# Moving the first stage's low-half subtractions from GpSimd to VectorE in a one-core decoder-layer kernel

## The chip, the cores and the metric

The kernel runs on one NeuronCore of one Trainium2 chip. The metric is the device time of one execution in microseconds (us). Engines are named as in the profile: PE is TensorE (PEld its weight loads), DVE is VectorE, ACT is ScalarE, POOL is GpSimd, and SP (SPq) is SyncE, which here only issues DMAs.

## The reference

One decoder layer on 512 tokens of width 1024, all in float32:

```
mod = silu(c) @ w_ada + b_ada                      # six vectors: sh1 sc1 gt1 sh2 sc2 gt2
h   = rms_norm(x, g_norm1) * (1 + sc1) + sh1
q_lat, kv_lat, k_rope, rq, rk, rv, rg = split(h @ w_in)   # 416 latent columns, then 4 x 512
x   = x + gt1 * (concat(mla(...), retention(...)) @ w_out)
h2  = rms_norm(x, g_norm2) * (1 + sc2) + sh2
x   = x + gt2 * peer(h2, w_query, sub_keys, expert_u, expert_v)
out = rms_norm(x, g_final)
```

## The kernel before

To keep float32 accuracy on TensorE, each operand of a wide product is split into a high half in the float32r format and a low half, low = value - high. A product is then three matmuls (`mm3`, L80): high by high, high by low, low by high (L81 to L83). `split` (L73) makes both halves of a weight tile: ACT copies the high half (L76), and the engine handed to it as `lo_engine` subtracts the low half (L77). The halves sit in two rotating buffers each, `hi` and `lo`.

The change lies in the first stage, `start` (L280). It goes over the eight 128-wide slices k of the model width, and for each k does the following.

1. `h_k(k)` (L231) loads two 512 KB rows of the modulation weights (`wadaT`, L131), multiplies each with silu(c) and sums on DVE (L133), adds the bias (L237) and forms the scale (L142). PE transposes and normalises the slice of x (L241), ACT applies scale and shift (L243) and makes the high half `hh` (L244), and L245 subtracts the low half `hl`.
2. `lat_load(k // 2)` (L247), for even k, loads and splits 832 columns of the latent weights; `lat_mm` (L252) multiplies four token blocks by 416 columns.
3. `wproj_load(0, k // 4)` (L257), for k = 0 and 4, loads and splits 1024 columns of the first wide projection, and `wproj_mm` (L262) multiplies. The first projection has `ci` = 0; the seven later ones call the same function with `ci` > 0.

Low halves are divided between DVE and POOL: `hl` always on POOL; latent weights on POOL for even and on DVE for odd loads; the first projection's load 0 on POOL and load 1 on DVE. After the loop come the rotary tables (`tables`, L177, some twenty small DVE operations), the evaluation of the latents (`ev_lat`, L297, with a power on POOL at L156) and the rotation of the first projection.

The weight rows stream through three buffers named `raw`, shared by the modulation rows and the later projections. In this part SP issues DMAs in program order; a load waits in SP's queue until the buffer that it fills is released, and all later loads wait behind it. The order of instructions on the other engines is laid out ahead of time by a planner that simulates the program with its own costs for each instruction, then each engine runs its queue in that order. The stages after `start` follow an order written out by hand:

```python
ORDER = "L m0! p1 d3 p2! m1 p3 d4 p4 d2 p5 p6 r0! r1! p7 r2 r3 X0 X1! d5! m2 g! m3 w0 X3 X2 h0 w1 q0 q1! h1 q2 q3"
```

Here L is `start`, p1 to p7 are the other projections, d the other modulation vectors (eight `wadaT` rows each), m and r the attention and retention blocks, w and q the output and query projections. A dense expert stage (about 700 to 1500 us) closes the kernel.

Of the kernel before, what the change touches and what calls it, by code (L numbers as in the profile page):

```python
# [8 lines left out]
F32 = mybir.dt.float32  # L9
# [11 lines left out]
NB = 4  # L21
# [27 lines left out]
def build(ctx: ExitStack, tc: tile.TileContext, A, out):  # L49
    nc = tc.nc  # L50
    V, S, P, T, G = nc.vector, nc.scalar, nc.gpsimd, nc.tensor, nc.sync
# [9 lines left out]
    def tpb():  # L61
        return ps.tile([128, 512], F32, name="tp", bufs=2)
# [7 lines left out]
    def raw_t():  # L70
        return st.tile([128, 1024], F32, name="raw", bufs=3)

    def split(raw, lo_engine, n=1024, pool=None, pre=""):  # L73
        hi = (pool or st).tile([128, 1024], R, name=pre + "hi", bufs=1 if pre == "f" else HB)
        lo = (pool or st).tile([128, 1024], R, name=pre + "lo", bufs=1 if pre == "f" else HB)
        S.activation(hi[:, :n], raw[:, :n], AF.Copy)  # L76
        lo_engine.tensor_sub(lo[:, :n], raw[:, :n], hi[:, :n].bitcast(F32))  # L77
        return hi, lo
# [17 lines left out]
    def w2(dt=F32):  # L96
        return fr.tile([128, 512], dt, name="w2", bufs=7)
# [10 lines left out]
    for hf in range(2):  # L108
        p = tpb()
# [19 lines left out]
    def mod1(w, k, raw=None):  # L129
        raw = raw_t() if raw is None else raw  # L130
        G.dma_start(raw, A["wadaT"][w, k])  # L131
        jk = st.tile([128, 1024], BF, name="junk", bufs=1)
        V.scalar_tensor_tensor(jk, raw, 1.0, csil, op0=OP.mult, op1=OP.mult,  # L133
                               accum_out=mod[:, w, k:k + 1])
# [6 lines left out]
    def mod_scale(w, g, ks=slice(0, 8)):  # L141
        V.scalar_tensor_tensor(mod[:, w, ks], mod[:, w, ks], 1.0, gn[:, g, ks], op0=OP.add, op1=OP.mult)  # L142
# [16 lines left out]
    hh = cp.tile([128, NB, 8, 128], R, name="hh")  # L159
    hl = cp.tile([128, NB, 8, 128], R, name="hl")  # L160
# [70 lines left out]
    def h_k(k):  # L231
        ks = slice(k, k + 1)
        mod1(0, k)
        k4 = k % 4
        mod1(1, k, kTt[:, 2 * k4 + 4:2 * k4 + 6, :].rearrange("p a c -> p (a c)") if k4 < 2 else
             vt[:, 2 * k4 - 4:2 * k4 - 2].rearrange("p a h d -> p (a h d)"))
        V.tensor_add(mod[:, 0:2, ks], mod[:, 0:2, ks], bada[:, 0:2, ks])  # L237
        mod_scale(0, 0, ks)
        p = tpb()
        for b in range(NB):  # L240
            T.matmul(p[:, b * 128:(b + 1) * 128], xts[b][:, k * 128:(k + 1) * 128], rdiag[:, b], start=True, stop=True)  # L241
        hf = w2()
        S.activation(hf, p, AF.Identity, scale=mod[:, 0, ks], bias=mod[:, 1, ks])  # L243
        S.activation(hh[:, :, k, :], hf.rearrange("p (b t) -> p b t", b=NB), AF.Copy)  # L244
        P.tensor_sub(hl[:, :, k, :], hf.rearrange("p (b t) -> p b t", b=NB), hh[:, :, k, :].bitcast(F32))  # L245

    def lat_load(kp):  # L247
        raw = blk[kp][:, 0:2, :].rearrange("p a c -> p (a c)")
        G.dma_start(raw[:, :832], A["w_in_a"][kp])
        return split(raw, V if kp % 2 else P, 832)  # L250

    def lat_mm(accs, w, k):  # L252
        for b in range(NB):
# [3 lines left out]
    def wproj_load(ci, kp):  # L257
        raw = raw_t() if ci else kTt[:, 2 * kp:2 * kp + 2, :].rearrange("p a c -> p (a c)")
        G.dma_start(raw, A["w_in_b"][ci, kp])
        return split(raw, P if kp % 2 == (ci > 0) else V)  # L260

    def wproj_mm(accs, w, k):  # L262
        rs = slice(k % 4 * 256, (k % 4 + 1) * 256)
# [8 lines left out]
    def wproj(ci, evac):  # L272
        accs = [acc(), acc()]
        for k in range(8):
            if k % 4 == 0:
                w = wproj_load(ci, k // 4)
            wproj_mm(accs, w, k)
        wproj_ev(accs, ci, evac)

    def start():  # L280
        la, pa = [acc(), acc(), acc(), ob()], [ab(), ab()]
        for k in range(8):
            h_k(k)
            if k % 2 == 0:
                w = lat_load(k // 2)
            lat_mm(la, w, k)
            if k % 4 == 0:
                wp = wproj_load(0, k // 4)
            wproj_mm(pa, wp, k)
        tables()  # L290
        G.dma_start(wuq, A["w_uq"])
        G.dma_start(wukv, A["w_ukv"])
        for b in range(NB):
            ev_lat(b, la[b])
        wproj_ev(pa, 0, ev_rope)
# [728 lines left out]
```

## Time and profile before

| quantity | before |
|---|---|
| median of 3 runs | 1621.45 us (1616.73 to 1622.6) |
| profiled execution | 1614.58 us, its span 1612.4 us, mean granted clock 0.98 |
| PE, DVE, POOL busy over the span | 94%, 82%, 56% |
| end of the first stage's matmuls | about 58.1 us |

The times of this table and of the rows below are of one profiled execution; the span is the part of its time from the first to the last instruction. Times within it are counted from the span's start.

### The profile page before, as it was taken

The page shows a single profiled execution, that of the slowest core. Times are in us where ns is not written, and L with a number is a line of the kernel's source. Part 1 is how long each engine was busy: PE and PEld are TensorE (multiplying, and loading weights), DVE is VectorE, ACT ScalarE, POOL GpSimd, SP SyncE. Part 2 cuts the span into 40 slices and gives each one's busy share as a digit, 9 for nine tenths or more (in the row PEclk, how much of TensorE's full clock was granted, in tenths as well). Part 3 has the DMA queues.
Part 4 walks back from the last instruction along what each step waited for, and adds up shares of the span by engine and source line. Part 5 has one row for each costly group of instructions (what it writes and reads, how often), then busy time and mean ns, then how long its engine had stood idle before and what let it go on. Part 6 is the DMA issues. An engine that isn't in the chain of part 4 may idle for free.

```text
span 1612.4 us, 24255 instructions
## 1 busy us (share of the span) xinstructions
PE 1520.5 (94%) x8977; PEld 1375.7 (85%) x8977; DVE 1318.9 (82%) x2315; ACT 625.3 (39%) x1009; POOL 910.3 (56%) x521
## 2 busy tenths in 40 slices
PE   6898999898799996899999999999999999999997
PEld 5788978798798995888889999999999999987876
DVE  7975654739989999989999988887878888888974
ACT  4433244445344555333333333333333333333332
POOL 4542651776440000127888877777787778865644
PEclk9999999999899997899999999999999999999999
DMA  9455350544333877859999998989988899888953
GB/s 357 154 183 185 122 183 13 196 158 133 117 118 101 250 233 216 272 174 316 344 318 331 330 331 312 322 299 316 325 298 319 309 321 330 305 302 294 318 203 105
DMA packets 196040, 395.62 MB, mean 245 GB/s; under 512 B 12241, under 2 KB 111569, under 8 KB 195922
## 3 DMA queue, kind: packets, MB, share of 16 engines
q1 hardware_dynamic: 157906, 257.22, 47.3%
q0 software_dynamic: 36864, 134.23, 23.6%
q10 hardware_dynamic: 1152, 2.62, 0.4%
q8 instruction: 70, 1.15, 0.3%
q14 instruction: 48, 0.39, 0.1%
HBM read 364.15 MB, written 29.88 MB: 244 GB/s over the span
## 4 chain that ended last, share of the span: by engine, by line
PE 57%; DVE 18%; DMA 12%; issue 7%; POOL 4%; ACT 1%; SPq 0%; DVEq 0%; POOLq 0%; ACTq 0%
PE ab L83 8%; PE ab L81 8%; PE ab L82 8%; PE acc L82 6%; PE acc L83 6%; PE acc L81 6%; DMA grow<-in_expert_u_dram,eidx 3%; DMA raw<-in_wadaT_dram 2%; PE tp L82 2%; PE tp L83 2%; PE tp L81 2%; DVE gacc L860 2%; DMA gtl<-Gd 1%; DVE junk L133 1%; DMA vraw<-in_expert_v_dram 1%
## 5 line engine op out<-in xcount | busy, mean ns | idle before, releaser
L77 POOL TENSOR_TENSOR vlo<-vraw,vhi 128x1024 fp32r<-128x1024 f32 x92 | 238.3, 2590 | 281.9 <-DVE v L596 206.0
L76 ACT ACTIVATE hi<-raw 128x1024 fp32r<-128x1024 f32 x204 | 216.3, 1060 | 379.1 <-PE ab L82 249.2
L83 PE MATMUL ab<-hh,lo 128*128 128x384 f32 x1024 | 346.5, 339 | 7.1 <-DVE lo L77 6.2
L81 PE MATMUL ab<-hh,hi 128*128 128x384 f32 x1024 | 346.0, 338 | 0.7 <-ACT ga L758 0.6
L82 PE MATMUL ab<-hl,hi 128*128 128x384 f32 x1024 | 345.2, 337 | 0.0
L77 POOL TENSOR_TENSOR lo<-raw,hi 128x1024 fp32r<-128x1024 f32 x71 | 185.9, 2621 | 156.6 <-ACT hi L76 148.7
L847 DVE SCALAR_TENSOR_TENSOR junk<-grow,h2n 128x1024 bf16<-128x1024 f32 x128 | 213.7, 1670 | 42.9 <-DMA grow<-in_expert_u_dram,eidx 41.3
L860 DVE SCALAR_TENSOR_TENSOR gacc<-grow,wsl,gacc 128x1024 f32<-128x1024 f32 x126 | 196.0, 1566 | 57.3 <-DMA grow<-in_expert_v_dram,eidx 57.0
L839 POOL DMA_INDIRECT grow<-in_expert_u_dram,eidx x128 | 184.3, 1440 | 81.0 <-DVE junk L847 28.6
L839 POOL DMA_INDIRECT grow<-in_expert_v_dram,eidx x128 | 181.5, 1418 | 42.4 <-issue 19.3
L77 DVE TENSOR_TENSOR lo<-raw,hi 128x1024 fp32r<-128x1024 f32 x133 | 183.6, 1381 | 24.8 <-ACT hi L76 24.8
L83 PEld LDWEIGHTS ab<-hh,lo 128*128 128x128 f32 x1024 | 192.9, 189 | 10.6 <-DVE lo L77 8.4
L81 PEld LDWEIGHTS ab<-hh,hi 128*128 128x128 f32 x1024 | 192.9, 188 | 4.7 <-ACT ga L758 1.0
L82 PEld LDWEIGHTS ab<-hl,hi 128*128 128x128 f32 x1024 | 193.0, 188 | 3.5
L824 ACT ACTIVATE wh<-wf 128x384 fp32r<-128x384 f32 x110 | 57.7, 526 | 266.4 <-issue 219.3
L82 PE MATMUL acc<-vlo,wh 128*128 128x512 f32 x330 | 129.7, 394 | 7.1 <-POOL vlo L77 4.9
L76 ACT ACTIVATE vhi<-vraw 128x1024 fp32r<-128x1024 f32 x110 | 115.6, 1051 | 50.4 <-DMA vraw<-in_expert_v_dram 47.8
L83 PE MATMUL acc<-vhi,wl 128*128 128x512 f32 x330 | 128.5, 390 | 0.0
L81 PE MATMUL acc<-vhi,wh 128*128 128x512 f32 x330 | 122.1, 390 | 0.1
L825 DVE TENSOR_TENSOR wl<-wf,wh 128x384 fp32r<-128x384 f32 x110 | 91.7, 834 | 13.6 <-ACT wh L824 13.5
L81 PE MATMUL acc<-hi,hh 128*128 128x256 f32 (+2 forms) x296 | 90.9, 315 | 4.5 <-ACT hi L76 2.0
L82 PE MATMUL acc<-lo,hh 128*128 128x256 f32 (+2 forms) x296 | 92.5, 313 | 1.6 <-DVE lo L77 0.8
(339 smaller groups left out, 3367.1 us busy)
## 6 DMA issues: line engine op xcount, KB each, us to landing
raw<-in_uT_dram SPq DMA_DIRECT2D x128, 512.0 KB
vraw<-in_expert_v_dram SPq DMA_DIRECT2D x110, 512.0 KB
Gd<-stg SPq DMA_DIRECT2D x12, 2048.0 KB
gtl<-Gd SPq DMA_DIRECT2D x32, 768.0 KB
raw<-in_wadaT_dram SPq DMA_DIRECT2D x40, 512.0 KB
raw<-in_w_query_dram SPq DMA_DIRECT2D x32, 512.0 KB
raw<-in_expert_v_dram SPq DMA_DIRECT2D x18, 512.0 KB
raw<-in_w_out_dram SPq DMA_DIRECT2D x16, 512.0 KB
```

The source lines that it names most:

```text
L76: S.activation(hi[:, :n], raw[:, :n], AF.Copy)
L77: lo_engine.tensor_sub(lo[:, :n], raw[:, :n], hi[:, :n].bitcast(F32))
L81: T.matmul(o, wh, rh, start=start, stop=False, skip_group_check=skip)
L82: T.matmul(o, wh, rl, start=False, stop=False, skip_group_check=skip)
L83: return T.matmul(o, wl, rh, start=False, stop=stop, skip_group_check=skip)
L133: V.scalar_tensor_tensor(jk, raw, 1.0, csil, op0=OP.mult, op1=OP.mult, accum_out=mod[:, w, k:k + 1])
L824: S.activation(wh, wf, AF.Copy)
L825: V.tensor_sub(wl, wf, wh.bitcast(F32))
L839: P.indirect_dma_start(out=r, out_offset=None, in_=A[table], in_offset=bass.IndirectOffsetOnAxis(ap=eidx[:, s:s + 1], axis=0))
L847: V.scalar_tensor_tensor(jk, r, 1.0, h2n, op0=OP.mult, op1=OP.mult, accum_out=asl[:, s:s + 1])
L860: V.scalar_tensor_tensor(g, r, wsl[:, s:s + 1], g, op0=OP.mult, op1=OP.add)
```

## The change

Eleven subtractions of the first stage are put on DVE: `hl` for all eight slices, the latent weights' loads 0 and 2, and load 0 of the first projection. The later projections keep their rule (odd loads on POOL, even ones on DVE).

```diff
@@ h_k
         S.activation(hh[:, :, k, :], hf.rearrange("p (b t) -> p b t", b=NB), AF.Copy)
-        P.tensor_sub(hl[:, :, k, :], hf.rearrange("p (b t) -> p b t", b=NB), hh[:, :, k, :].bitcast(F32))
+        V.tensor_sub(hl[:, :, k, :], hf.rearrange("p (b t) -> p b t", b=NB), hh[:, :, k, :].bitcast(F32))
@@ lat_load
         G.dma_start(raw[:, :832], A["w_in_a"][kp])
-        return split(raw, V if kp % 2 else P, 832)
+        return split(raw, V, 832)
@@ wproj_load
         G.dma_start(raw, A["w_in_b"][ci, kp])
-        return split(raw, P if kp % 2 == (ci > 0) else V)
+        return split(raw, P if ci > 0 and kp % 2 else V)
```

## Rows read from the trace of the kernel before

**Rows 1.** Page, chain that ended last: shares of the span by engine

```profile
PE 57%; DVE 18%; DMA 12%; issue 7%; POOL 4%; ACT 1%; SPq 0%; DVEq 0%; POOLq 0%; ACTq 0%
```

**Rows 2.** Windows: stretch, its length, busy time per engine, granted clock, DMA share, GB/s

```profile
18.50:58.10 39.60, 34.81 (x232) 33.74 (x232) 37.55 (x65) 14.81 (x25) 21.51 (x10) 1.00 0.72 281
12.00:25.00 13.00, 8.12 (x42) 7.33 (x43) 9.70 (x12) 4.32 (x8) 7.49 (x4) 1.00 1.02 397
25.00:50.00 25.00, 23.26 (x164) 22.81 (x163) 24.58 (x41) 11.34 (x15) 14.45 (x7) 1.00 0.88 337
50.00:58.10 8.10, 8.06 (x56) 7.85 (x54) 6.54 (x21) 3.44 (x9) 1.62 (x1) 1.00 0.01 3
58.10:180.00 121.90, 111.26 (x853) 101.59 (x854) 84.08 (x177) 43.41 (x109) 50.93 (x41) 0.97 0.53 175
```

**Rows 3.** Waits of PE, 16 to 58.1 us: total, times, longest

```profile
PE tp L241 <- ACT w L243: 2.9, 3, 1.6
PE acc L83 <- POOL hl L245: 1.7, 1, 1.7
PE ab L82 <- POOL lo L77: 1.2, 1, 1.2
```

**Rows 4.** Waits of SP's DMA queue, 45 to 62 us

```profile
SPq L131 <- DVE lo L77: 13.4, 1, 13.4
```

**Rows 5.** Lines of POOL by form, 14 to 56 us: busy us, mean ns, idle before

```profile
L245 POOL TENSOR_TENSOR hl<-w,hh 128x512 fp32r<-128x512 f32 x8 | 15.8, 1984 | 13.4 <-ACT hh L244 13.4
L77 POOL TENSOR_TENSOR lo<-blk,hi 128x832 fp32r<-128x832 f32 x2 | 4.4, 2216 | 5.0 <-ACT hi L76 5.0
L77 POOL TENSOR_TENSOR lo<-kTt,hi 128x1024 fp32r<-128x1024 f32 x1 | 3.4, 3357 | 0.0
```

**Rows 6.** One line's instructions (L391): ns least/median/most, first and last start

```profile
L391 DVE TENSOR_TENSOR w<-ab,t4k x8: 681/686/692, 161.3 to 210.0; 128x512 f32<-128x512 f32 x8
```

**Rows 7.** Timeline of DVE: start us, length us, instruction, idle before it

```profile
25.02 0.15 DVE L142 SCALAR_TENSOR_TENSOR mod<-mod,gn 128x1 f32<-128x1 f32 x1
...
26.41 0.16 DVE L237 TENSOR_TENSOR mod<-mod,bada 128x2 f32<-128x2 f32 x1
...
26.68 1.22 DVE L133 SCALAR_TENSOR_TENSOR junk<-raw,csil 128x1024 bf16<-128x1024 f32 x1
...
32.44 1.02 DVE L77 TENSOR_TENSOR lo<-blk,hi 128x832 fp32r<-128x832 f32 x1
...
35.80 0.16 DVE L142 SCALAR_TENSOR_TENSOR mod<-mod,gn 128x1 f32<-128x1 f32 x1
...
40.60 1.94 DVE L142 SCALAR_TENSOR_TENSOR mod<-mod,gn 128x1 f32<-128x1 f32 x1
42.46 1.21 DVE L77 TENSOR_TENSOR lo<-kTt,hi 128x1024 fp32r<-128x1024 f32 x1
...
49.86 0.16 DVE L142 SCALAR_TENSOR_TENSOR mod<-mod,gn 128x1 f32<-128x1 f32 x1
```

**Rows 8.** Timeline of POOL

```profile
18.39 3.36 POOL L77 TENSOR_TENSOR lo<-kTt,hi 128x1024 fp32r<-128x1024 f32 x1
21.70 2.25 POOL L245 TENSOR_TENSOR hl<-w,hh 128x512 fp32r<-128x512 f32 x1
...
40.05 2.47 POOL L77 TENSOR_TENSOR lo<-blk,hi 128x832 fp32r<-128x832 f32 x1 [0.54 <-ACT hi L76]
```

**Rows 9.** Lines of DVE by form, 12 to 50 us

```profile
L133 DVE SCALAR_TENSOR_TENSOR junk<-kTt,csil 128x1024 bf16<-128x1024 f32 x4 | 6.9, 1731 | 1.0 <-DMA kTt<-in_wadaT_dram 0.9
L237 DVE TENSOR_TENSOR mod<-mod,bada 128x2 f32<-128x2 f32 x8 | 6.1, 763 | 0.2
L133 DVE SCALAR_TENSOR_TENSOR junk<-vt,csil 128x1024 bf16<-128x1024 f32 x4 | 5.9, 1463 | 0.1
L142 DVE SCALAR_TENSOR_TENSOR mod<-mod,gn 128x1 f32<-128x1 f32 x8 | 3.0, 380 | 0.2
```

**Rows 10.** Timeline of ACT

```profile
16.97 1.05 ACT L76 ACTIVATE hi<-kTt 128x1024 fp32r<-128x1024 f32 x1
...
25.27 0.78 ACT L243 ACTIVATE w<-tp,mod 128x512 f32<-128x512 f32 x1 [6.74 <-DVE mod L142]
...
35.99 0.78 ACT L243 ACTIVATE w<-tp,mod 128x512 f32<-128x512 f32 x1 [1.99 <-DVE mod L142]
36.80 0.64 ACT L244 ACTIVATE hh<-w 128x512 fp32r<-128x512 f32 x1
```

**Rows 11.** Chain that ended last, in order of time: start us, length us, what

```profile
10.57 7.43 DMA raw<-in_wadaT_dram
18.03 1.32 DVE junk L133
```

## The prediction

> **What bounds the kernel now.** I read the chain that ended last first. Over the whole span PE sets 57% of it, DVE 18%, DMA 12% [rows 1]; so the whole is a matmul kernel with stretches in which something else feeds PE too late. The change touches only the stretch before 58.1 us, so next come the windows. From 18.5 us, when the first high half is there, to 58.1 us, when the last matmul of the stage ends, PE is busy 34.81 of 39.60 us [rows 2]: 4.8 us of idle time is all that a better supply of the stage can give back. The reader should see in the same table that DVE is busy 24.58 of 25 us between 25 and 50 us, POOL 14.45; DMA is full (share 1.02) from 12 to 25 us and idle (0.01) after 50 us.
>
> The waits of PE say who was late [rows 3]: 1.2 us for a POOL low half of a weight, 1.7 us for POOL's first `hl`, and 2.9 us for ACT's scaled slice (L243). ACT is not the cause of the last: its own wait before L243 is for L142 on DVE, 6.74 us for slice 1 [rows 10]. So PE waits for POOL once at the start, and otherwise for the chain of DVE's modulation sums.
>
> Last, SP's queue: a load of `wadaT` waits 13.4 us until DVE has made the low half of the second projection's weights [rows 4]. No load starts until this stage's last matmuls free the `hi` and `lo` buffers. What the stage gains is therefore handed on: the next weights start earlier by as much.
>
> **The change, part by part.** *Taken from POOL:* eight `hl` at 15.8 us, two latent halves at 4.4 and one projection half at 3.4, together 23.6 us [rows 5]. These eleven are all that POOL does in that window. Freeing POOL is worth nothing by itself.
>
> *Put on DVE:* the 832-column half costs 1.02 us and the 1024-column one 1.21 [rows 7]. A 128x512 subtraction out of SBUF into float32r is not in the trace; by the line through 832 and 1024 columns it is 0.70 us, and a 512-column multiplication with one input in PSUM takes 0.69 [rows 6]. I take 0.69. Sum: 8 x 0.69 + 2 x 1.02 + 1.21 = 8.8 us more work on an engine that seems full.
>
> *Taken from DVE: its waits inside instructions.* The two-element bias addition L237 takes 0.16 us when left alone, and so does L142 [rows 7]. But L142 at 40.60 takes 1.94 us and ends at 42.54, when POOL's subtraction that began at 40.05 ends (42.52) [rows 7, 8]. The grouped lines give the whole: L237 6.1 us in place of 8 x 0.16, so 4.8 lost; L142 3.0 in place of 1.3, 1.7 lost; L133 into `kTt`'s and `vt`'s rows 6.9 and 5.9 in place of 4 x 1.22 each, 2.0 and 1.0 lost [rows 7, 9]. That is 9.5 us of standing still. If none of it came from POOL it stays (0); at most it all goes. Because the one with its POOL partner in the rows ends within 0.02 us of it, I take all 9.5. DVE then has 8.8 - 9.5 = -0.7 us: about as busy as before, with work in place of waiting.
>
> The Trainium skill has the rule for this row, "SBUF — State Buffer", section "Who interferes with whom": a DVE instruction with two SBUF inputs and a GpSimd instruction that reads SBUF exclude each other, and whichever comes second waits for the whole of the other. The trace agrees (1.94 us against 0.16).
>
> *Pace of DVE and of PE.* From slice 1 to slice 7, L142 goes from 25.02 to 49.86 [rows 7], 4.14 us a slice. In these six slices DVE would gain six `hl` and one latent half, 6 x 0.69 + 1.02 = 5.2 us, and lose most of the waits that fall there, about 7 of the 9.5 (the long one into `kTt`'s row and one L237 lie before): 24.84 + 5.2 - 7 = 23.0, 3.8 us a slice. PE needs 34.81 / 8 = 4.35 us a slice. DMA needs 1024 KB of rows, 208 of latent and 128 of projection weights, 1.39 MB, at 397 GB/s [rows 2] 3.5 us. So once slice 1 is there, PE is last, and neither DVE nor DMA. SP issues its loads earlier, since `raw` is released earlier, but the DMA is full and lands them no sooner than that 3.5 us a slice.
>
> *The start.* ACT has the projection's high half at 18.02 [rows 10], and DVE then makes its low half until 19.2; POOL took until 21.75 [rows 8]. On DVE follow the row of slice 1 that landed at 18.03 [rows 11] until 20.4, `hl` of slice 0 until 21.1 (POOL: 23.95), the second row until 22.3, L237 and L142 until 22.6. L142 ended at 25.17 [rows 7], so slice 1 comes 2.5 us earlier. Of PE's waits the 1.2 and 1.7 go; PE finishes slice 0 near 22.2 and waits some 1.5 for slice 1. Later, the 1.6 us before slice 7's transposes goes, since it hung on the L142 at 40.60 [rows 3, 7]. New: each `hl` can stand behind a 1.22 us row sum on DVE, which PE partly hides by doing the high-half products first; and a latent half stands between row sums too. I put these at 0 to 2 us and take 1.1. Gain of the stage: 2.5 + 1.6 - 1.1 = 3.0 us, at least 2.1 without surprises and never over 4.8.
>
> *Afterwards.* The tables follow on DVE and end before PE does, so they stay hidden under PE's last slices; if not, the next weights' low half is late by the remainder, under 2 us. The 3.0 us are then carried on one to one: 1614.58 - 3.0 = 1611.6 for an execution like the profiled one, which was 6.9 us below the median of the runs shown; on that median, 1621.45 - 3.0 = 1618.4 us.
>
> **The rivals.** *A: DVE becomes the bound of the stage (slower).* Place: DVE's queue between L142 of a slice and its `hl`. ACT needs from 35.96 to 37.44 for L243 and L244 [rows 7, 10], 1.5 us. If the planner puts `hl` right behind L142, DVE stands still that long in each slice: 3.8 + 1.5 = 5.3 us against PE's 4.35. L142 of slice 7 then ends at 22.6 + 6 x 5.3 = 54.4, its high half is there at 55.9, and PE needs another 3.9 to 59.8, against 58.1: +1.7 us, 1623.2. It decides from a period of 5.0, a wait of 1.2 us a slice. For it: the order is laid out by simulated costs. Against it: before, row sums stand between the steps of neighbouring slices. Its far end is that the waits don't go at all: L142 of slice 7 at 50.0 + 8.1, the end at 58.1 + 1.5 + 3.9 = 63.5, +5.4 us, 1626.9.
>
> This far end is also what a rule that speaks against the change would give: the Trainium skill, "Perfetto Trace Analysis", section "Optimizing Scalar/DVE Operations", says that with DVE saturated, moving work off it to GpSimd may make sense, so that moving work onto it would not; the same place adds that the shared read port may undo it. The trace has both: DVE 98% busy, and 9.5 us of that a wait.
>
> *B and C: the plan behind the stage falls out differently.* The planner sees 8.8 us of work change engine and may reorder the stretch after 58.1 us, in which `raw` loads, row sums and projections alternate. PE is idle there for 121.90 - 111.26 = 10.6 us [rows 2]. B: a better order gives most of that back on top of the 3.0, 1608 to 1613. C: a worse one loses turns of the three `raw` buffers; one lost turn is a load's 7.43 us and its row sum's 1.2 [rows 11], 8.6 us, less the 3.0: 1627; two turns 1636. Nothing in the profile says which; the chain after 58.1 us is DMA, DVE and PE in turn, so it can go either way.
>
> That the change doesn't do what it says can hardly be: POOL has no other work in the stage.
>
> **Chances.** Forecast 0.48; A 0.20; B 0.14; C 0.18. A measurement of this kernel tells about 0.5% (8 us) from no change. The forecast and A lie within it; of B some 0.14 and a little of the forecast's upper end by scatter are faster; C is slower in most cases, with a little of A's far end. Faster 0.17, same 0.65, slower 0.18. The likeliest case alone spans 1616 to 1621; with A, most of B and one lost turn the range is 1608 to 1629.
>
> **What would show it.** In the changed profile: no POOL subtraction before 58 us; every L237 and L142 of the stage near 0.16 us; the new 128x512 form near 0.69; L142 of slice 1 near 22.6 and PE's last L83 of the stage near 55; PE idle in the stage about 2 us. The prediction is wrong if L237 stays near 0.76, if DVE has idle time in front of `hl` (A), or if the stage ends 3 us earlier and the kernel's time doesn't follow (B, C).

## Result: 11 us faster, where 3 were forecast

| | before | after |
|---|---|---|
| median of 6 runs each | 1619.09 us (1615.32 to 1623.26) | 1608.09 us (1605.46 to 1610.04) |
| ratio, 95% interval | | 0.9931 [0.9912, 0.9949] |
| profiled execution, its span | 1614.58 us, 1612.4 us | 1608.14 us, 1606.2 us |
| end of the stage's last L83 into `ab` | 58.06 us | 53.95 us |

By the ratio the change takes off 11.2 us, with an interval of 8.3 to 14.2: faster by 0.7%. Two repeats gave 7.9 and 8.6 us (below). Ratios here are those of the undisturbed timed runs and not of the medians, so the two differ a little.

The stage after the change, first as windows (stretch, its length, busy time of PE, PEld, DVE, ACT, POOL, granted clock, DMA share, GB/s), then the waits of PE from 16 to 58.1 us, then those of SP's queue:

```profile
18.50:54.00 35.50, 33.86 (x231) 33.15 (x229) 31.45 (x77) 14.90 (x24) 0.07 (x1) 1.00 0.77 302
25.00:50.00 25.00, 25.00 (x177) 24.94 (x176) 22.64 (x55) 12.01 (x16) 0.00 (x0) 1.00 0.82 322
```

```profile
PE tp L241 <- ACT w L243: 1.9, 2, 1.5
PE acc L82 <- DVE lo L77: 0.8, 1, 0.8
PE acc L81 <- ACT hi L76: 0.7, 1, 0.7
```

```profile
SPq L131 <- DVE lo L77: 12.5, 1, 12.5
```

PE is idle for 35.50 - 33.86 = 1.64 us of the stage, where it was 4.79 [rows 2], and not at all from 25 to 50 us. Both waits for POOL [rows 3] are gone. DVE has 2.4 us to spare from 25 to 50 us, with more to do.

Not all of the 4.1 us by which the stage ends earlier is gained in it. ACT begins the first projection's high half at 16.97 us before [rows 10] and at 16.32 us after. This moment follows the landing of the first loads, which the change does not touch; in other executions of the changed kernel's stage it lies between 17.16 and 18.09 us. So the stage is counted from there (ACT's line of after, then the windows of before and of after):

```profile
16.32 1.04 ACT L76 ACTIVATE hi<-kTt 128x1024 fp32r<-128x1024 f32 x1
```

```profile
16.97:58.06 41.09, 35.97 (x240) 34.71 (x240) 37.98 (x65) 16.30 (x27) 23.04 (x11) 1.00 0.74 286
16.32:53.95 37.63, 35.86 (x240) 34.96 (x240) 33.01 (x78) 16.42 (x27) 0.02 (x1) 1.00 0.78 309
```

The same 240 matmuls take 41.09 and 37.63 us, 3.5 us less; nearly all of it is idle time of PE, 5.12 and 1.77 us.

The lines of DVE by form, 12 to 50 us, show why (busy us, mean ns, idle before):

```profile
L245 DVE TENSOR_TENSOR hl<-w,hh 128x512 fp32r<-128x512 f32 x8 | 5.5, 686 | 0.4 <-ACT hh L244 0.4
L133 DVE SCALAR_TENSOR_TENSOR junk<-kTt,csil 128x1024 bf16<-128x1024 f32 x4 | 4.9, 1220 | 1.1 <-DMA kTt<-in_wadaT_dram 1.1
L133 DVE SCALAR_TENSOR_TENSOR junk<-vt,csil 128x1024 bf16<-128x1024 f32 x4 | 4.9, 1219 | 0.0
L237 DVE TENSOR_TENSOR mod<-mod,bada 128x2 f32<-128x2 f32 x8 | 1.3, 160 | 0.2
L142 DVE SCALAR_TENSOR_TENSOR mod<-mod,gn 128x1 f32<-128x1 f32 x8 | 1.2, 155 | 0.1
```

Against [rows 9], the same four lines stand still 9.6 us less: 4.8 in L237, 1.8 in L142, 2.0 and 1.0 in L133. The eight `hl` cost 0.686 us each and wait 0.4 us in all. A fifth instruction stood still too, the conversion of the positions for the rotary tables (L181, before and then after):

```profile
48.51 1.25 DVE L181 CAST posf<-pos 128x4 f32<-128x4 int32 x1
```

```profile
42.73 0.16 DVE L181 CAST posf<-pos 128x4 f32<-128x4 int32 x1
```

The timelines of DVE, of POOL and of PE at its last matmul of the stage, after the change:

```profile
18.49 1.22 DVE L77 TENSOR_TENSOR lo<-kTt,hi 128x1024 fp32r<-128x1024 f32 x1
19.63 0.69 DVE L245 TENSOR_TENSOR hl<-w,hh 128x512 fp32r<-128x512 f32 x1
...
22.72 0.15 DVE L142 SCALAR_TENSOR_TENSOR mod<-mod,gn 128x1 f32<-128x1 f32 x1
...
44.25 0.16 DVE L142 SCALAR_TENSOR_TENSOR mod<-mod,gn 128x1 f32<-128x1 f32 x1
```

```profile
10.74 1.02 POOL L156 TENSOR_TENSOR rx<-rx,mhalf 128x4 f32<-128x4 f32 x1 [9.68 <-DVE rx L155]
53.93 0.70 POOL L156 TENSOR_TENSOR rl<-rl,mhalf 128x2 f32<-128x2 f32 x1 [42.17 <-DVE rl L155]
56.01 2.59 POOL L77 TENSOR_TENSOR lo<-raw,hi 128x1024 fp32r<-128x1024 f32 x1 [1.38 <-ACT hi L76]
```

```profile
53.67 0.28 PE L83 MATMUL ab<-hi,hl 128*128 128x256 f32 x1
```

The first `hl` is ready at 20.3 us instead of 23.95 [rows 8]; L142 of slice 1 starts 2.3 us earlier than in [rows 7], that of slice 7 5.6 us earlier, 0.65 us of each by the earlier start. POOL is idle for 42 us and then begins the next projection's half before 58 us, because the stage ends sooner.

The chain of the whole kernel, shares by engine, has PE 6 points lower and "issue" 5 higher than [rows 1], far more than 11 us of the span. Three of its pieces in the first 60 us (start, length, what) stand below it:

```profile
PE 51%; DVE 19%; issue 12%; DMA 10%; POOL 5%; ACT 1%; DVEq 0%; POOLq 0%; SPq 0%; ACTq 0%
```

```profile
10.74 1.02 POOL rx L156
11.76 42.13 issue
53.93 0.71 POOL rl L156
```

The chain now passes through POOL's two powers, and as POOL waits for nothing else that the profile shows, the whole stage between them (42.13 us, 2.6% of the span) is put down as "issue". A share of the chain can move without a change of what is done; the stage is read from its windows.

So the stage ends 4.1 us earlier, 3.5 of it gained in the stage, and the kernel 11. The rest was looked for by dividing the kernel at marks. From the stage's end to the first L561 (query stage) before takes 257.8 us and after 257.05: the gain is carried on. The first L784 (one-hots from which the expert gates `Gd` are built) starts at 497.1 and 492.2 us, 4.9 us earlier; the spans end at 1612.4 and 1606.2, 6.2 us apart. (The profiled execution of before lies 4.5 us below its median, so this pair shows only part of the 11.)

What does differ there is the order of the queues. Row by row, the queues of both kernels differ in some rows just behind the stage, up to 81 us, and then agree until about 635 us, while `Gd` is built. The rows up to 81 us bring no time that shows: from the stage's end to the first L784 it takes 439.0 us before and 438.3 after, and 440.2 and 438.3 in two repeats (e4, e11). From 635 to some 970 us DVE, and for parts of it PE, ACT and SP, run in another order. The first place on SP's queue (- before, + after; `raw` takes expert `u` rows here):

```diff
 L743 DMA raw<-in_uT_dram 128x1024 x2
 L801 DMA Gd<-stg 128x32x128 x6
-L743 DMA raw<-in_uT_dram 128x1024 x2
-L801 DMA Gd<-stg 128x32x128
+L743 DMA raw<-in_uT_dram 128x1024
+L801 DMA Gd<-stg 128x32x128
+L743 DMA raw<-in_uT_dram 128x1024
 L811 DMA gtl<-Gd 128x12x128
```

The theory is then: the stage gives 3 to 4 us through the waits inside DVE instructions, and the planner's other order behind 635 us gives about 3 more. The rivals: the stage alone gives all of it, in a way that the profile doesn't show; or one part of the change does it all.

### The profile page after: what moved, and what is told of

It reads as the page before. It is cut to its first block, busy times and chain, and to the rows that moved or that the text cites. A ratio compares the mean times of both kernels' runs of the same rounds, so it can differ in the third digit from the quotient of the medians.

```text
span 1606.2 us, 24258 instructions
## 1 busy us (share of the span) xinstructions
PE 1516.5 (94%) x8977; PEld 1373.1 (85%) x8977; DVE 1311.2 (82%) x2326; ACT 623.6 (39%) x1009; POOL 877.0 (55%) x510
## 4 chain that ended last, share of the span: by engine, by line
PE 51%; DVE 19%; issue 12%; DMA 10%; POOL 5%; ACT 1%; DVEq 0%; POOLq 0%; SPq 0%; ACTq 0%
PE ab L83 7%; PE ab L81 7%; PE ab L82 7%; PE acc L82 6%; PE acc L83 5%; PE acc L81 5%; DMA grow<-in_expert_u_dram,eidx 3%; DVE gacc L860 2%; POOL grow L839 2%; DMA grow<-in_expert_v_dram,eidx 2%; PE tp L82 2%; PE tp L83 2%; PE tp L81 2%; DVE lo L77 2%; POOL vlo L77 2%
## 5 line engine op out<-in xcount | busy, mean ns | idle before, releaser
L77 POOL TENSOR_TENSOR vlo<-vraw,vhi 128x1024 fp32r<-128x1024 f32 x92 | 242.6, 2637 | 284.6 <-ACT vhi L76 283.5
L83 PE MATMUL ab<-hh,lo 128*128 128x384 f32 x1024 | 346.0, 338 | 3.7 <-DVE lo L77 2.4
L860 DVE SCALAR_TENSOR_TENSOR gacc<-grow,wsl,gacc 128x1024 f32<-128x1024 f32 x126 | 200.9, 1603 | 59.6 <-DMA grow<-in_expert_v_dram,eidx 59.5
L847 DVE SCALAR_TENSOR_TENSOR junk<-grow,h2n 128x1024 bf16<-128x1024 f32 x128 | 199.3, 1557 | 43.7 <-DMA grow<-in_expert_u_dram,eidx 42.6
L839 POOL DMA_INDIRECT grow<-in_expert_v_dram,eidx x128 | 171.4, 1339 | 54.8 <-DVE gacc L860 29.3
L83 PEld LDWEIGHTS ab<-hh,lo 128*128 128x128 f32 x1024 | 192.4, 188 | 7.2 <-DVE lo L77 5.0
L83 PE MATMUL acc<-vhi,wl 128*128 128x512 f32 x330 | 129.3, 393 | 0.0
L825 DVE TENSOR_TENSOR wl<-wf,wh 128x384 fp32r<-128x384 f32 x110 | 99.5, 905 | 15.8 <-ACT wh L824 15.7
```

The source lines that it names most:

```text
L83: return T.matmul(o, wl, rh, start=False, stop=stop, skip_group_check=skip)
L825: V.tensor_sub(wl, wf, wh.bitcast(F32))
L839: P.indirect_dma_start(out=r, out_offset=None, in_=A[table], in_offset=bass.IndirectOffsetOnAxis(ap=eidx[:, s:s + 1], axis=0))
L847: V.scalar_tensor_tensor(jk, r, 1.0, h2n, op0=OP.mult, op1=OP.mult, accum_out=asl[:, s:s + 1])
L860: V.scalar_tensor_tensor(g, r, wsl[:, s:s + 1], g, op0=OP.mult, op1=OP.add)
```

## The experiments

Kernels of one group ran on one chip and share its runs of before: the first four (before 1617.72 us, 33 runs), then the three cut kernels with e8 (1619.02 us, 17 runs), then the last three (1617.75 us, 22 runs).

**e1: the new late order without the change.** Of all eleven subtractions only `hl` of slice 7 is moved. That small edit alone leads the planner to the late order of the changed kernel.

```diff
-        P.tensor_sub(hl[:, :, k, :], hf.rearrange("p (b t) -> p b t", b=NB), hh[:, :, k, :].bitcast(F32))
+        (V if k == 7 else P).tensor_sub(hl[:, :, k, :], hf.rearrange("p (b t) -> p b t", b=NB), hh[:, :, k, :].bitcast(F32))
```

> Kernel of before with one of the eleven subtractions moved to VectorE, hl of slice 7. From the first rows of the first stage to the building of Gd the order of the engines' queues is nearly that of before; from the building of Gd on (some 640 us) it is the order of after, row for row. Theory P (the late order is worth what the first stage does not explain, some 6 us of the 11): 5 to 7 us faster than before, the stage ending within 1 us of before's 58.1. Theory S (the stage alone, carried on to the end with interest): 0 to 1 us faster.

Measured: 1614.97 us (12 runs), ratio 0.9981 [0.9967, 0.9996], that is 3.1 us faster (0.6 to 5.3). Its stage gains nothing: the last matmul ends at 58.9 us and the first L784 starts at 498.6 us, later than before's 497.1. So the 3.1 us lie behind, with the late order; they are fewer than the 5 to 7 expected of the late order and more than the 0 to 1 expected without it. The trace shows part of the place. The 40 us behind the expert indices (`eidx`, L670), windows with the columns of above, of before and then of e1:

```profile
715.10:755.10 40.00, 37.18 (x188) 33.19 (x187) 32.95 (x35) 11.89 (x16) 31.99 (x19) 1.00 0.96 336
```

```profile
715.00:755.00 40.00, 38.50 (x196) 34.60 (x195) 36.52 (x37) 13.43 (x18) 34.39 (x19) 1.00 0.95 338
```

and the wait of PE for POOL's `vlo` in the same stretches, before and e1:

```profile
PE acc L82 <- POOL vlo L77: 2.8, 3, 1.4
```

```profile
PE acc L82 <- POOL vlo L77: 1.5, 1, 1.5
```

In the new order PE does 196 matmuls there instead of 188 and waits 1.3 us less for a weight half.

**e2: the whole change, meant to have the old late order.** Four multiplications by 1.0 of two columns are added in slice 5, which turns the planner back.

```diff
-        mod_scale(0, 0, ks)
+        mod_scale(0, 0, ks); [V.tensor_scalar(mod[:, 0:2, ks], mod[:, 0:2, ks], 1.0, None, op0=OP.mult) for _ in range(4 if k == 5 else 0)]
```

> Kernel of after with four extra multiplications by one on two elements in slice 5, which shift the planner: from the building of Gd on its order is that of before but for 12 rows of VectorE. Theory P: the stage ends near 54.5 us and the whole is 3.5 to 5 us faster than before, not 11. Theory S: 9 to 11 us faster, as after.

Measured: 1617.68 us (12 runs), 1.0001 [0.9983, 1.0019]. A miss: the late order is before's but for some rows of DVE and four of PE, but the order in and just behind the stage changed too, up to 98 us. The projection's last matmul ends at 55.8 us, but twenty matmuls of the latents now stand behind it, and the stage's last one ends at 59.6 us, later than before's 58.1:

```profile
59.24 0.34 PE L83 MATMUL ob<-hi,hl 128*128 128x416 f32 x1
```

The first L784 starts at 500.5 us, 3.4 later than before. So the stage as a whole gains nothing here, and the run says nothing on the late order alone. It does say that a worse order (C) is as near at hand as a better one.

**e3: the three weight halves alone,** `hl` left on POOL; the late order is before's but for one row of DVE.

```diff
-        return split(raw, V if kp % 2 else P, 832)
+        return split(raw, V, 832)
...
-        return split(raw, P if kp % 2 == (ci > 0) else V)
+        return split(raw, P if ci > 0 and kp % 2 else V)
```

> Only the three weight low halves (latent loads 0 and 2, first projection load 0) on VectorE, the eight hl on GpSimd; late order as before's, row for row. Theory P: faster by what its stage ends earlier, 1 to 3 us. Theory S: more than twice that.

Measured: 1616.09 us (12 runs), 0.9995 [0.9979, 1.001]. L237 still takes 4.2 us in all. The stage ends at 56.1 us; counted from ACT's first projection half (17.79 us) it takes 38.3 us, against 41.1 before and 37.6 after. Three subtractions give 2.8 of the stage's 3.5 us, and no time that can be told from none.

**e4: the changed kernel again,** on the chip of e1 to e3.

> The changed kernel unaltered, beside the other three on one chip: both theories 11 us faster than before (8 to 14).

Measured: 1610.15 us (10 runs), 0.9951 [0.9934, 0.9968]: 7.9 us faster (5.2 to 10.7).

**e5, e6: before and after, cut behind the output projection.** They leave out the last steps (normalisation, query, top-k, experts) and write x as it stands behind the mixer, so the late order can't act.

```diff
-ORDER = "L m0! p1 d3 p2! m1 p3 d4 p4 d2 p5 p6 r0! r1! p7 r2 r3 X0 X1! d5! m2 g! m3 w0 X3 X2 h0 w1 q0 q1! h1 q2 q3"
+ORDER = "L m0! p1 d3 p2! m1 p3 d4 p4 d2 p5 p6 r0! r1! p7 r2 r3 X0 X1! d5! m2 g! m3 w0 X3 X2 w1"
...
-    spm.close()
+    spm.close(); [G.dma_start(out[b * 128:(b + 1) * 128, :], blk[b][:, 2:4, :].rearrange("p a c -> p (a c)")) for b in range(NB)]; pr_.close(); pf.close(); ptk.close(); return
```

> Kernel of before cut off after the output projection: normalisation, query, top-k and experts are left out, x after the mixer is written out. Up to the cut the order of its queues is that of before. Both theories: the baseline of the next two, some 330 to 350 us; nothing is to be told from it alone.

> Kernel of after cut in the same place, the order up to the cut that of after. Theory P (stage worth 3 to 5 us, the rest of the gain from the order laid out behind): 3 to 5 us less than the cut kernel of before. Theory S (all from the stage and what directly follows): 8 to 11 us less.

Measured, as ratios to the full kernel before: 0.1963 [0.1957, 0.1969] (317.96 us, 5 runs) and 0.1928 [0.192, 0.1936] (311.55 us, 6 runs). The difference of 0.0035, with the half-intervals 0.0006 and 0.0008 put together to 0.0010, is 5.7 us of 1619, give or take 1.6. So the first 318 us hold most of the gain, but not 8 to 11 us of it. Part of the 5.7 may be the clock: the profiled executions of the two have a mean granted clock of 0.964 and 0.99.

**e7: the cut changed kernel with POOL kept busy.** Eight POOL subtractions of 128x512 are added beside `hl`, into a tile that nobody reads; PE, DVE, ACT and SP keep the order of e6 row for row.

```diff
-        V.tensor_sub(hl[:, :, k, :], hf.rearrange("p (b t) -> p b t", b=NB), hh[:, :, k, :].bitcast(F32))
+        V.tensor_sub(hl[:, :, k, :], hf.rearrange("p (b t) -> p b t", b=NB), hh[:, :, k, :].bitcast(F32)); P.tensor_sub(twin, hh[:, :, k, :].bitcast(F32), hh[:, :, k, :].bitcast(F32))
```

> The cut kernel of after with eight subtractions of 128x512 added on GpSimd, each as soon as the slice's high half is there, into a tile that nobody reads; the order of all other engines is that of the cut kernel of after. If VectorE's waits were GpSimd's doing, L237 and L142 of the stage go back from 0.16 to several of 1 us, VectorE is 6 to 9 us longer in the stage, and the stage ends 3 to 7 us later than in the cut kernel of after. If they were not, the time is that of the cut kernel of after within 0.5 us.

Measured: 0.1942 [0.1933, 0.1951] (315.25 us, 6 runs); against e6 0.0014, give or take 0.0012, or 2.3 us (0.3 to 4.2). The stage ends at 58.6 us instead of 55.0; counted from ACT's first projection half (18.11 and 17.34 us) it takes 40.5 us instead of 37.7, 2.8 us more. The windows of the stage, first e6 and then e7:

```profile
18.50:55.00 36.50, 36.03 (x238) 35.45 (x236) 32.49 (x77) 15.25 (x25) 0.00 (x1) 1.00 0.79 307
```

```profile
18.50:58.60 40.10, 36.04 (x240) 34.51 (x239) 38.48 (x75) 16.04 (x26) 12.98 (x8) 1.00 0.74 289
```

In these windows PE's busy time is the same, its idle time goes from 0.47 to 4.06 us, a part of it by the later start. Lines of DVE by form in e7, 12 to 58 us:

```profile
L245 DVE TENSOR_TENSOR hl<-w,hh 128x512 fp32r<-128x512 f32 x8 | 6.3, 788 | 0.4 <-ACT hh L244 0.4
...
L237 DVE TENSOR_TENSOR mod<-mod,bada 128x2 f32<-128x2 f32 x8 | 2.1, 264 | 0.2
L142 DVE SCALAR_TENSOR_TENSOR mod<-mod,gn 128x1 f32<-128x1 f32 x8 | 2.1, 259 | 0.1
```

Two of its stalls, on DVE's timeline and on POOL's:

```profile
28.03 0.99 DVE L142 SCALAR_TENSOR_TENSOR mod<-mod,gn 128x1 f32<-128x1 f32 x1
...
39.47 2.06 DVE L133 SCALAR_TENSOR_TENSOR junk<-kTt,csil 128x1024 bf16<-128x1024 f32 x1
```

```profile
27.26 1.74 POOL L245 TENSOR_TENSOR twin<-hh 128x512 f32<-128x512 f32 x1 [5.92 <-ACT hh L244]
...
38.97 1.48 POOL L245 TENSOR_TENSOR twin<-hh 128x512 f32<-128x512 f32 x1 [2.50 <-ACT hh L244]
```

L142 ends at 29.02 us, POOL's subtraction, which began before it, at 29.00. L133 takes 0.84 us more than its 1.22, and POOL ends 0.98 us after L133 began. So the waits come from POOL's subtractions, with no product depending on their results; fewer of them fall on L237 and L142 than before, since the twins come at other moments. By the Trainium skill, "SBUF — State Buffer", section "Who interferes with whom", the second of two such instructions waits for the whole of the first: these rows agree.

**e8: most of the change without the new late order.** On top of the change, `hl` of slices 0 and 5 go back to POOL. The late order was expected to be before's but for 29 rows of DVE; by the trace PE and SP keep before's order only to 722 and 819 us, and up to 870 us 251 places of PE's queue hold another row than before. It is a third order, neither before's nor after's.

```diff
-        V.tensor_sub(hl[:, :, k, :], hf.rearrange("p (b t) -> p b t", b=NB), hh[:, :, k, :].bitcast(F32))
+        (P if k in (0, 5) else V).tensor_sub(hl[:, :, k, :], hf.rearrange("p (b t) -> p b t", b=NB), hh[:, :, k, :].bitcast(F32))
```

> Kernel of after with hl of slices 0 and 5 left on GpSimd (six hl and all three weight halves on VectorE). From the building of Gd on its order is that of before but for 29 rows of VectorE. Theory P: 2 to 4 us faster than before, by the stage alone. Theory S: 6 to 9 us faster.

Measured: 1614.17 us (12 runs), 0.9974 [0.9958, 0.9989]: 4.2 us faster (1.8 to 6.8). The stage ends at 54.7 us; counted from ACT's first projection half (16.37 us) it takes 38.3 us, which is 2.8 of the 3.5 us gained. With most of the stage's gain and without the new order behind, the kernel gains about 4 us, and not 8 to 11.

**e9, e10: the whole change, both late orders, with the same extra work.** Sixteen unneeded ACT copies of scores are added in the query stage, at head 3 (e9: behind the building of `Gd`, PE takes before's order) or at head 7 (e10: after's order row for row).

```diff
-                    S.activation(Sc[b][:, h], p4[:, i], AF.Copy)
+                    S.activation(Sc[b][:, h], p4[:, i], AF.Copy); [S.activation(Sc[b][:, h], p4[:, i], AF.Copy) for _ in range(8 if pr == 1 and h == 3 else 0)]
```

(h == 7 in e10.)

> Kernel of after with 16 copies of scores made again on ScalarE in the query stage (head 3). The order of TensorE is after's up to the building of Gd and before's from there on, VectorE's from there before's but for 4 rows. If the late order is worth some 3 us beside a stage worth 4 to 6: 3 to 6 us faster than before, and 3 us slower than its twin with head 7. If the late order is worth nothing: 8 to 11 us faster, like the twin.

> The same 16 extra copies at head 7: the order of TensorE is after's row for row, and all late rows too. Both theories: as after, 8 to 11 us faster than before, less what the copies cost (0 to 3 us).

Measured: e9 1617.9 us (12 runs), 1.0007 [0.9994, 1.002]; e10 1610.69 us (11 runs), 0.9953 [0.9936, 0.9969]. The 0.0054 between them, 8.7 us, are not all of the order: the copies cost time in e9 where they cost none in e10. The score matmuls of the query stage (ns least, median, most; first and last start), e9 and then e10:

```profile
L561 PE MATMUL acc<-subk,w x128: 270/275/377, 312.9 to 447.6; 128*128 128x128 f32 x128
```

```profile
L561 PE MATMUL acc<-subk,w x128: 270/275/377, 313.0 to 441.4; 128*128 128x128 f32 x128
```

They take 134.7 us in e9 and 128.4 in e10 (before 128.0). Without these 6.3 us some 2.4 remain, and the interval of the difference is 3.4 us either way: in the direction of the theory, and not a test of it by itself. The stretch behind `eidx`, e9 and e10, goes with the order again:

```profile
717.40:757.40 40.00, 38.37 (x194) 34.37 (x193) 32.80 (x35) 11.88 (x16) 31.95 (x19) 1.00 0.95 335
```

```profile
711.00:751.00 40.00, 39.16 (x198) 34.94 (x197) 35.29 (x35) 13.43 (x18) 33.05 (x19) 1.00 0.95 339
```

**e11: the changed kernel a third time,** on the chip of e9 and e10.

> The changed kernel unaltered, for the scale of the two on the same chip: 8 to 11 us faster than before.

Measured: 1609.35 us (5 runs), 0.9947 [0.9934, 0.996]: 8.6 us faster (6.5 to 10.7).

**The late part over all profiles.** From the first L784 to the end of the span, the five profiles without after's order (before's in before, and but for some rows in e3, e2 and e9; e8's third order) take 1115.3 to 1118.3 us, mean 1117.2; the five with after's order (after, e1, e4, e10, e11) 1111.4 to 1114.9, mean 1113.8. Every one of the second group is below every one of the first, 3.4 us apart in the mean: near e1's 3.1 by time.

The two groups stand apart at marks on the way as well. From the first L784 to `eidx` it takes 217.6 to 218.1 us without after's order and 216.3 to 216.8 with it; to the first L860 (which sums gathered expert `v` rows, from 1113 to 1128 us on) 623.2 to 627.4 and 620.6 to 622.3, means 4.4 us apart. So the difference comes about where the orders differ, and nothing is added behind. In the 40 us behind `eidx` PE does 186 to 194 matmuls without after's order and 196 to 198 with it, and waits 1.6 to 3.3 us and 0.8 to 1.5 us for `vlo`.

## Why the prediction was right and wrong

**DVE's waits go with POOL's work: right.** 9.5 us of waits were to go and 9.6 went; 8.8 us of subtractions were to come and 5.5 + 2 x 1.02 + 1.22 = 8.8 came, 0.686 us for the form that the trace of before didn't have (0.69 taken). The sum missed L181, which gave back 1.1 us more. e7 shows that POOL's work is the cause.

**DVE does not become the bound (rival A): right.** L142 goes from slice 1 to slice 7 in 21.53 us, 3.6 us a slice (3.8 forecast), while PE has 33.86 / 8 = 4.2 us of work a slice. Moving work onto an engine that was 98% busy helped, because part of "busy" was standing still. The Trainium skill, "Perfetto Trace Analysis", section "Optimizing Scalar/DVE Operations", says that with DVE saturated, moving work to GpSimd may make sense, and that it might not help because the two share a read port. This case agrees with the reservation: work moved the other way made the stage 3.5 us shorter. No run here moves more work from DVE to POOL.

**The stage's gain: right in what it comes from, about 0.5 us too small.** The waits for POOL went, and PE's idle time fell to 1.64 us (about 2). The gain was to be 3.0 us. The stage ends 4.1 us earlier in the profiled pair, but 0.65 of that lies ahead of it. Counted from ACT's first projection half, six profiles with the whole change (after, e4, e6, e9, e10, e11) take 37.6 to 37.7 us and before 41.1, all at a granted clock of 1.00, the upper of the two levels: 3.4 to 3.5 us. (e5, with before's stage, takes 41.8 us, at a mean clock of 0.96.) The timed pair e5 and e6 has 5.7, give or take 1.6.

That L142 of slice 1 came at 22.72 us (22.6 forecast) is partly luck. Counted from the same mark it came 1.65 us earlier, not 2.5; the planner put a row sum of slice 2 in front of it:

```profile
21.57 1.22 DVE L133 SCALAR_TENSOR_TENSOR junk<-raw,csil 128x1024 bf16<-128x1024 f32 x1
```

The rest of the stage's gain came in the later slices: L142 of slice 7 came 5.0 us earlier by that count.

**"Carried on one to one": the step that failed.** Up to the building of `Gd` it held (4.9 us earlier at the first L784). Behind it the planner laid out another order, some 580 us after the last instruction that was changed, and that is worth about 3 us: e1 has the order without the stage's gain and is 3.1 us faster, e8 has most of the stage's gain without the new order and is 4.2 faster, and the late parts of all profiles differ by 3.4. The prediction did have "the plan behind the stage falls out differently" as rival B, with the range of times that came out, but it put it at the wrong place (from 58.1 to 180 us, for the 10.6 us of idle time there), where the order changed in some rows up to 81 us only and no time came of it, and gave it 0.14 only. The order of a planner can't be read from the profile of before, and e2 shows that another one can take back all that the change gives; what was wrong was to give the unchanged order so large a share.

**The numbers.** The forecast was 1618.4 us from a median of 1621.45. Of the 10.3 us to 1608.09, 2.4 are the median of before itself, which came out at 1619.09 over six runs; 0.5 are the stage, and about 3.1 the late order. The 4.3 left over are scatter or something not found. By the two repeats the change takes off 7.9 (5.2 to 10.7) and 8.6 us (6.5 to 10.7). Stage and order together give 3.5 + 3.4 = 6.9 us by the traces and 5.7 + 3.1 = 8.8 by the timed pieces: both lie within these intervals, and the first stays below the 8.3 to 14.2 of the first result.

**What stays open.** Which rows of the new late order bring the 3 us was not tried; the fewer waits for `vlo` are part of what is seen, not shown to be the cause. No run has exactly the changed stage and exactly before's late order without other work added.

## What to carry to other kernels

Read a busy engine for instructions that take longer than their own size asks (0.76 us for two elements): time lost in them comes back when the engine that holds them up is relieved, even if the work goes to the waiting engine. Where a planner lays out the queues, a local edit may change the order far behind it, so compare the queues of both kernels to the end, in the traces and not only in the plan, before the whole difference is put down to the edit. A variant that gets the new order by another tiny edit (e1), and a kernel cut before the place where the orders part (e5, e6), separate the two. Count a stage from an event at its start rather than from the span's start: here the first loads landed up to 1.8 us apart in the same stage, half as much as the gain.

## What the runs showed that was not expected

A POOL subtraction holds up more than the small sums. One step of the rotary tables on DVE takes 2.42 us where it overlaps the POOL subtraction from 56.01 to 58.60 us shown above; the copy behind it, which is no smaller, takes 0.21. In the kernel before, the same two are the other way round: the step took 0.22 us and the copy, which met POOL's subtraction, 2.42. DVE and POOL before, then DVE after:

```profile
58.63 0.22 DVE L211 TENSOR_SCALAR ssr<-ssr 128x128 f32<-128x128 f32 x1
...
61.04 2.42 DVE L212 COPY ccr<-ccr 128x128 f32<-128x128 f32 x1
```

```profile
60.44 2.94 POOL L77 TENSOR_TENSOR lo<-raw,hi 128x1024 fp32r<-128x1024 f32 x1 [1.03 <-issue]
```

```profile
56.27 2.42 DVE L211 TENSOR_SCALAR ssr<-ssr 128x128 f32<-128x128 f32 x1
58.61 0.21 DVE L212 COPY ccr<-ccr 128x128 f32<-128x128 f32 x1
```

So a collision of 2.2 us is there before and after, at the start of the next projection, which keeps its odd halves on POOL.

The granted clock of the 40 us in which the queues part is higher with the new order in most profiles, before and then after, and last e11, which has the new order too:

```profile
645.00:685.00 40.00, 34.67 (x222) 32.13 (x222) 39.50 (x152) 15.79 (x26) 6.01 (x2) 0.89 0.88 274
```

```profile
640.00:680.00 40.00, 34.62 (x229) 32.06 (x229) 40.00 (x156) 16.75 (x27) 6.16 (x2) 0.94 0.89 284
```

```profile
641.40:681.40 40.00, 34.64 (x223) 31.98 (x223) 40.00 (x157) 16.01 (x26) 5.79 (x2) 0.89 0.90 285
```

With 0.94 PE does 229 matmuls in it instead of 222 in the same busy time. But DVE is busy all the while, and e11 has 0.89, like before, and the shortest late part of all (1111.4 us). So the gain of the late order does not need the higher clock.
